# An encoder block on one core: seven products for more pieces of the third group, and adding transfers that read from memory

## The chip, the cores and the metric

The kernel runs on 1 core of one Trainium2 chip. The metric is the device time in microseconds of one execution; lower is better.

## The reference

One layer of a streaming encoder for 256 tokens with 2048 features, all in float32:

```python
x = x + 0.5 * swiglu(rms_norm(x, ffn1_norm), ffn1_w_up, ffn1_w_down)     # FFN1, d_ff = 5632
h = rms_norm(x, mix_norm); proj = h @ w_in                               # HGRN2 and RG-LRU branches
...
x = x + merged @ w_out
x = x + cross_attention(rms_norm(x, xattn_norm), rms_norm(mem, mem_norm), wq, wkv, wo)
x = x + 0.5 * swiglu(rms_norm(x, ffn2_norm), ffn2_w_up, ffn2_w_down)     # FFN2, d_ff = 5632
return rms_norm(x, final_norm)

def swiglu(h, w_up, w_down):
    gate, up = jnp.split(h @ w_up, 2, axis=-1)
    return (jax.nn.silu(gate) * up) @ w_down
```

The change touches the two FFNs and the start of the first.

## The kernel before

**Products in three matmuls.** TensorE multiplies in a float32 of reduced precision (fp32r). Each operand is split in two parts, h (the rounded value) and l (what rounding took off), and a product is h·h + l·h + h·l: three matmuls of 128x128 by 512 columns (`three`). A plain split of a 128x2048 piece of weights (1 MB, tile `raw`) is an ACT copy into `h` and a DVE subtraction into `l` (`split`).

**The FFN's tiles.** The 5632 hidden columns go in 11 groups of 512 (g = 0 to 10). The up weights of a group come in 8 pieces (p = 0 to 7), each with gate and up columns for two of x's 16 row blocks; x's matching operands are `pairs[p]`. A piece takes 8 products in the plain or the "mixed" form. The "fast" form is Strassen's scheme in Winograd's arrangement with 7 products; it needs sums and differences of x (made once, `sums`, on DVE and ACT) and of the weights: DVE makes `td` (three subtractions: 1024, 512 and 512 columns), then both `raw` (1536 columns) and `td` (twice 1024 columns) are split, into `h`, `l` and `th`, `tl`. Before the change groups 1 and 2 alternate mixed and fast; groups 3 to 10 go in the order p = 1, 3, 0, 4, 2, 6, 5, 7 with 0 and 6 mixed. After each group stand 2 or 4 "down" pieces, 24 matmuls each, which multiply hidden columns of earlier groups and add to the residual x.

**Adding transfers.** In groups 3 to 10 a mixed piece's split is kept off DVE (kind "added"): ACT writes -raw, rounded, into `l`, and a DMA from POOL's queue adds raw to it in SBUF, which leaves what rounding took off. `begin_added` does this one piece ahead, before the piece between; `prepare` later copies `raw` into `h`:

```python
sp.dma_start(raw, src)
act.activation(l, raw, ACT.Copy, scale=-1.0)
nc.gpsimd.dma_start(l, raw, accum_op=ALU.add)
```

**Order and buffers.** `weights` makes each piece ready two pieces before PE uses it. SP issues all loads in order. Each engine works through its instructions in the order that a scheduler fixes when the kernel is built, and an instruction that waits keeps all behind it on its engine. `raw`, `h` and `l` have three buffers each (a fast piece takes two of `h`), `td` and `tl` one; `slots` are 24 buffers of 128x1024 that hold x's operands, hidden operands and small things. The first 8 pieces have an order written out by hand (`tc.manual_schedule`); the lists `head` and `rest` put x's loads, x's sums and the residual's loads between the pieces.

**The start.** ACT's queue loads the gains (`vt`), PE runs 16 products of ones to be warm, ACT scales x by the gain into `xg`, and `split` makes x's operands from that.

Of the kernel before, what the change touches and what calls it, by code (L numbers as in the profile page):

```python
# [8 lines left out]
F32 = mybir.dt.float32  # L9
# [4 lines left out]
P = 128  # L14
T = 256
# [26 lines left out]
def ffn_order():  # L42

    out, down = [("plain", 0, p) for p in range(8)], [("down", 0, 1, c, 0) for c in range(4)]
    for g in range(1, NG):
        if g < 3:  # L50
            out += [(("mixed", "fast")[p % 2], g, p) for p in (0, 1, 2, 3, 5, 4, 7, 6)]
        else:
            out += [("mixed" if p in (0, 6) else "fast", g, p) for p in (1, 3, 0, 4, 2, 6, 5, 7)]
        if g > 2 and g % 2:
            down = [("down", g - 2, 2, c, b) for c in range(4) for b in (g - 2, g - 1)]
        n = 2 if g < 3 else 4
        out, down = out + down[:n], down[n:]
    return out + [("down", NG - 2, 2, c, b) for c in range(4) for b in (NG - 2, NG - 1)]
# [3 lines left out]
def block_kernel(ctx: ExitStack, tc: tile.TileContext, xT, xin, memT, vec, gfin, bgate, lruw, wu1, wd1, win, wv,  # L62
# [33 lines left out]

    vt = const.tile([P, NVEC], F32, name="vt")
    small_n = VEC["ident"][0]
    act.dma_start(vt[:, :small_n], vec[:, :small_n])

    def col(name, i=0, n=1):
        a = VEC[name][0] + i
        return vt[:, a:a + n]
# [1 line left out]
    ones = const.tile([P, P], F32, name="ones")  # L105
    dve.memset(ones, 1.0)
    warm = bank("warm")
    for _ in range(16):
        pe.matmul(warm[:, :P], ones, ones, start=True, stop=True)
    eps = const.tile([P, 1], F32, name="eps")  # L110
    act.activation(eps, ones[:, :1], ACT.Copy, scale=EPS)
# [6 lines left out]

    def split(h, l, raw):
        done["high"] = act.activation(h, raw, ACT.Copy).ins  # L120
        dve.tensor_tensor(out=l, in0=raw, in1=h.bitcast(F32), op=ALU.subtract)  # L121
# [64 lines left out]
    def begin_added(src):  # L186

        raw = rawp.tile([P, 2048], F32, name="raw", tag="raw")
        l = lp.tile([P, 2048], F32R, name="l", tag="l")
        sp.dma_start(raw, src)  # L190
        act.activation(l, raw, ACT.Copy, scale=-1.0)
        nc.gpsimd.dma_start(l, raw, accum_op=ALU.add)
        return raw, l

    def prepare(src, kind, cuts=1):
# [17 lines left out]
        dve.tensor_tensor(out=two[0], in0=raw[:, None, :512].broadcast_to([P, 2, 512]), in1=two[1], op=ALU.subtract)  # L213
        dve.tensor_tensor(out=td[:, 1024:1536], in0=raw[:, 1024:1536], in1=td[:, :512], op=ALU.subtract)
        dve.tensor_tensor(out=td[:, 1536:], in0=raw[:, 1536:], in1=td[:, 1024:1536], op=ALU.subtract)
        h, l = split_tiles()
        split(h[:, 512:], l[:, 512:], raw[:, 512:])
        th = hp.tile([P, 2048], F32R, name="h", tag="h")
# [184 lines left out]
    BOTH = [2, 4]  # L403
    xd = []

    def operand_pairs(src, gain, q, xg, out):

        for a in src:
            i = len(out)
            g = xg[:, i * 512:(i + 1) * 512]  # L410
            for z in range(2):
                act.activation(g[:, z * T:][:, :T], a[:, z * T:(z + 1) * T], ACT.Copy,
                               scale=col(gain, 4 * q + 2 * i + z))
            h, l = slot(F32R, "xh"), slot(F32R, "xl")
            split(h[:, :512], l[:, :512], g)
# [8 lines left out]
        def sums():  # L424
            s = slot(name="xs")
            for i, ((h, l), less) in enumerate(out):
                a = [xg[:, i * 512 + j * P:][:, :P] for j in range(4)]

                def made(h, l, n, at, terms):
                    o = [s[:, at + j * P:][:, :P] for j in range(n)]  # L430
                    for j, (x, y, op) in enumerate(terms(o)):
                        dve.tensor_tensor(out=o[j], in0=x, in1=y, op=op)
                    split(h, l, s[:, at:at + n * P])

                if less:
                    made(*less, 2, 0, lambda o: ((a[0], a[1], ALU.subtract), (a[2], a[3], ALU.subtract)))
                if i or 2 * q in BOTH:
                    if not i:
# [15 lines left out]
    def part(pair, i, n):  # L454
        return [v[:, i * n:(i + 1) * n] for v in pair]
# [9 lines left out]
    def ffn(name, pairs, sq, then, begin=(), sums=()):  # L465
# [38 lines left out]
        for at, e in enumerate(order):  # L504
# [3 lines left out]
            if kind != "down":  # L508
# [3 lines left out]
                for i, (a, b, n) in enumerate(PRODUCTS[kind]):  # L512
                    u = uses[g, n]
                    if u[0] == (p, i):
                        accs[n] = bank()
                    own, less = pairs[p]
                    products.append((accs[n], part(own, a, P) if a >= 0 else part(less, -1 - a, P), part(w[b // 4] if fast else w, b % 4, 512),
                                     u[0] == (p, i), u[-1] == (p, i)))
# [53 lines left out]
    def head_x(p):  # L572

        q = p // 2
        if p % 2 == 0:
            xq[q] = slot(name="xf"), slot(name="xg"), []
        src, xg, out = xq[q]
        a = p % 2 * 512
        sp.dma_start(src[:, a:a + 512], xT[:, p * 512:(p + 1) * 512])
        sums = operand_pairs([src[:, a:a + 512]], "ffn1_norm", q, xg, out)  # L580
        if p % 2:
            sums1.append(sums)
        pairs1.append(out[-1])
# [51 lines left out]
    def to_mix(c, t):  # L635
        sq2.add(c, [t])
        if t == 0:
            return
        if c == 0:
            with tc.issue_after(done["residual"]):  # L640
# [539 lines left out]
```

## Time and profile before

| what | value |
|---|---|
| median of 3 runs | 2455.2 us (2454.61 to 2457.94) |
| the profiled execution's own time | 2454.05 us |
| its span, first to last instruction | 2452.3 us |
| PE, DVE, ACT busy | 2436.5, 1887.3, 1402.5 us |
| granted TensorE clock | 0.999 |
| HBM read | 472.07 MB, 193 GB/s over the span |
| FFN1, middle, FFN2 | about 0 to 700, 700 to 1745, 1745 to 2452 us |

Profile rows give the line of the source (L449: line 449 of the kernel before), the engine, the operation, output and input tiles, a count, the busy time, the mean of one and then the idle time of the engine ahead of them with what ended it. In the FFN, L449 is h·h, L450 l·h (x's low part) and L452 h·l (the weights' low part). `l<-raw` on POOL's queue is the adding transfer. Ends of matmuls are modelled; a row of them shows their rate better than the length of one.

### The profile page before, as it was taken

The page shows a single profiled execution, that of the slowest core. Times are in us where ns is not written, and L with a number is a line of the kernel's source. Part 1 is how long each engine was busy: PE and PEld are TensorE (multiplying, and loading weights), DVE is VectorE, ACT ScalarE, POOL GpSimd, SP SyncE. Part 2 cuts the span into 40 slices and gives each one's busy share as a digit, 9 for nine tenths or more (in the row PEclk, how much of TensorE's full clock was granted, in tenths as well). Part 3 has the DMA queues.
Part 4 walks back from the last instruction along what each step waited for, and adds up shares of the span by engine and source line. Part 5 has one row for each costly group of instructions (what it writes and reads, how often), then busy time and mean ns, then how long its engine had stood idle before and what let it go on. Part 6 is the DMA issues. An engine that isn't in the chain of part 4 may idle for free.

```text
span 2452.3 us, 30292 instructions
## 1 busy us (share of the span) xinstructions
PE 2436.5 (99%) x12250; PEld 2032.2 (83%) x12250; DVE 1887.3 (77%) x2015; ACT 1402.5 (57%) x1399; POOL 28.1 (1%) x36
## 2 busy tenths in 40 slices
PE   9999999999999999999999999999999999999998
PEld 8787888888888888888888888888888788888887
DVE  7989999999865757577665676556689999999995
ACT  8566666666564454477434554555555666666664
POOL 0000000000000000000000000000000000000000
PEclk9999999999999999999999999999999999999999
DMA  7567777777655544546555555444555777777774
GB/s 288 196 219 228 239 232 234 238 238 239 229 187 189 174 173 179 177 168 230 189 189 178 210 197 189 172 172 155 189 189 185 230 240 238 240 240 234 233 237 153
DMA packets 75308, 509.69 MB, mean 208 GB/s; under 512 B 8352, under 2 KB 8608, under 8 KB 15264
## 3 DMA queue, kind: packets, MB, share of 16 engines
q1 hardware_dynamic: 69840, 473.06, 54.7%
q0 software_dynamic: 4608, 33.56, 6.6%
q8 instruction: 96, 1.57, 0.3%
q10 hardware_dynamic: 720, 1.13, 0.1%
q14 instruction: 44, 0.36, 0.0%
HBM read 472.07 MB, written 2.10 MB: 193 GB/s over the span
## 4 chain that ended last, share of the span: by engine, by line
PE 92%; DMA 3%; DVE 3%; issue 1%; ACT 1%; SPq 0%; ACTq 0%; POOLq 0%; DVEq 0%
PE acc L452 16%; PE acc L449 16%; PE acc L450 16%; PE acc L231 11%; PE acc L252 8%; PE acc L253 8%; PE acc L255 8%; PE acc L235 5%; DMA raw<-wu 2%; DVE l L121 1%; DMA l<-raw 1%; PE acc L488 1%; ACT h L120 1%; PE acc L389 1%; DVE tl L121 0%
## 5 line engine op out<-in xcount | busy, mean ns | idle before, releaser
L121 DVE TENSOR_TENSOR l<-raw,h 128x2048 fp32r<-128x2048 f32 (+2 forms) x420 | 873.9, 2084 | 327.0 <-ACT h L120 322.4
L120 ACT ACTIVATE h<-raw 128x2048 fp32r<-128x2048 f32 (+2 forms) x420 | 734.8, 1752 | 534.7 <-PE acc L253 205.3
L449 PE MATMUL acc<-h,xh 128*128 128x512 f32 x1280 | 500.3, 391 | 4.3 <-ACT h L120 4.2
L450 PE MATMUL acc<-h,xl 128*128 128x512 f32 x1280 | 497.7, 389 | 0.0
L120 ACT ACTIVATE h<-td 128x1024 fp32r<-128x1024 f32 x224 | 235.8, 1055 | 241.4 <-DVE td L213 98.8
L121 DVE TENSOR_TENSOR tl<-td,h 128x1024 fp32r<-128x1024 f32 x224 | 273.1, 1221 | 82.6 <-ACT h L120 51.4
L252 PE MATMUL acc<-h,ops 128*128 128x512 f32 x832 | 326.9, 393 | 0.0
L253 PE MATMUL acc<-h,ops 128*128 128x512 f32 x832 | 324.3, 390 | 0.0
L449 PEld LDWEIGHTS acc<-h,xh 128*128 128x128 f32 x1280 | 240.3, 188 | 59.0 <-ACT h L120 8.4
L450 PEld LDWEIGHTS acc<-h,xl 128*128 128x128 f32 x1280 | 240.4, 188 | 49.1
L231 PE MATMUL acc<-ops,h 128*128 128x512 f32 x1152 | 277.9, 393 | 0.3
L449 PE MATMUL acc<-h,hidop 128*128 128x512 f32 x704 | 275.9, 392 | 0.0
L450 PE MATMUL acc<-h,hidop 128*128 128x512 f32 x704 | 274.4, 390 | 0.0
L231 PEld LDWEIGHTS acc<-ops,h 128*128 128x128 f32 x1152 | 211.9, 188 | 42.8 <-DVE ops L292 0.9
L452 PE MATMUL acc<-l,xh 128*128 128x512 f32 x832 | 217.7, 389 | 0.0
L255 PE MATMUL acc<-l,ops 128*128 128x512 f32 x832 | 206.1, 390 | 0.0
L452 PE MATMUL acc<-l,hidop 128*128 128x512 f32 x704 | 188.4, 389 | 0.0
L255 PEld LDWEIGHTS acc<-l,ops 128*128 128x128 f32 x832 | 156.2, 188 | 32.4
L452 PEld LDWEIGHTS acc<-l,xh 128*128 128x128 f32 x832 | 156.0, 188 | 32.5 <-DVE l L121 0.2
L252 PEld LDWEIGHTS acc<-h,ops 128*128 128x128 f32 x832 | 156.3, 188 | 32.3
L253 PEld LDWEIGHTS acc<-h,ops 128*128 128x128 f32 x832 | 156.3, 188 | 31.6
L452 PEld LDWEIGHTS acc<-l,hidop 128*128 128x128 f32 x704 | 132.2, 188 | 27.7
(218 smaller groups left out, 2360.0 us busy)
## 6 DMA issues: line engine op xcount, KB each, us to landing
raw<-wu SPq DMA_DIRECT2D x172, 1024.0 KB, 5.3
raw<-wd SPq DMA_DIRECT2D x88, 1024.0 KB, 4.8
raw<-win SPq DMA_DIRECT2D x40, 1024.0 KB, 4.8
l<-raw POOLq DMA_DIRECT2D x32, 1024.0 KB, 11.0
raw<-wg SPq DMA_DIRECT2D x32, 1024.0 KB, 4.8
raw<-wab SPq DMA_DIRECT2D x16, 1024.0 KB, 4.8
raw<-wout SPq DMA_DIRECT2D x16, 1024.0 KB, 4.8
raw<-wq SPq DMA_DIRECT2D x16, 1024.0 KB, 4.8
```

Source lines behind the costliest of these rows:

```text
L120: done["high"] = act.activation(h, raw, ACT.Copy).ins
L121: dve.tensor_tensor(out=l, in0=raw, in1=h.bitcast(F32), op=ALU.subtract)
L231: pe.matmul(acc, h[:, k * P:(k + 1) * P], xs[k], start=k == 0, stop=False)
L235: done["product"] = pe.matmul(acc[:, :T], l[:, k * P:(k + 1) * P], xs[k][:, :T], start=False, stop=k == KT - 1).ins
L252: pe.matmul(accs[t], x[:, t * P:][:, :P], h[j], start=first and j == 0, stop=False)
L253: pe.matmul(accs[t], x[:, T + t * P:][:, :P], h[j], start=False, stop=False)
L255: done["product"] = pe.matmul(accs[t], x[:, t * P:][:, :P], l[j], start=False, stop=last and j == 3).ins
L389: pe.transpose(accs[m // 2][:, m % 2 * T + t * P:][:, :P], tile[:, t * 512 + m * P:][:, :P], ident)
L449: pe.matmul(acc, ah, bh, start=start, stop=False)
L450: pe.matmul(acc, al, bh, start=False, stop=False)
L452: pe.matmul(acc, ah, bl, start=False, stop=stop)
L488: pe.transpose(acc[:, z * T + t * P:][:, :P], hid[t][:, (2 * y + z) * P:][:, :P], ident)
```

## The change

- Group 2 takes the order and forms of groups 3 to 10: two mixed pieces and six fast ones.
- An adding transfer reads the weights from HBM and no longer from `raw`. It is begun by the preparation of the piece two ahead of it, after that piece's first splits, and its `h` is made there too, as two tiles of 1024 columns in `slots`. All mixed pieces are done so but (1,0), (1,6) and (2,0), so two of group 1 and one of group 2 are new: 38 adding transfers where 32 were.
- The gains' load is cut in two (16 columns first), 13 warm products stand where 16 did, x's first operand is made directly from x and the gain, and the second half of each of x's scalings goes to DVE in the first FFN. x's sums for pairs 2 and 4 are made at pieces 16 and 17 (the two downs after group 1). `parameters` is held back behind the latest weight copy.

```diff
-        if g < 3:
+        if g < 2:
             out += [(("mixed", "fast")[p % 2], g, p) for p in (0, 1, 2, 3, 5, 4, 7, 6)]
...
-    act.dma_start(vt[:, :small_n], vec[:, :small_n])
+    first_n = VEC["mix_norm"][0]
+    for a, b in ((0, first_n), (first_n, small_n)):
+        act.dma_start(vt[:, a:b], vec[:, a:b])
...
-    for _ in range(16):
+    for _ in range(13):
...
-            kind = "fast" if e[0] == "fast" else "added" if e[0] == "mixed" and e[1] > 2 else "plain"
+            kind = "fast" if e[0] == "fast" else "plain"
+            if e[0] == "mixed" and e[1:] not in ((1, 0), (1, 6), (2, 0)):
+                kind = "added"
...
-            if plan and plan[0][2] == "added":
-                begun.append(begin_added(plan[0][1]))
-            ahead.append((k, prepare(src, kind, 4 if i < 4 else 1)))
+            begin = [p[1] for p in plan[1:2] if p[2] == "added"]
+            ahead.append((k, prepare(src, kind, 4 if i < 4 else 1, begin)))
...
         act.activation(l, raw, ACT.Copy, scale=-1.0)
-        nc.gpsimd.dma_start(l, raw, accum_op=ALU.add)
-        return raw, l
+        nc.gpsimd.dma_start(l, src, accum_op=ALU.add)
+        h = [slot(F32R, "wh") for _ in range(2)]
+        for i in range(2):
+            done["high"] = act.activation(h[i], raw[:, i * 1024:(i + 1) * 1024], ACT.Copy).ins
+        return h, [l[:, :1024], l[:, 1024:]]
...
         if kind == "added":
-            raw, l = begun.pop(0)
-            h = hp.tile([P, 2048], F32R, name="h", tag="h")
-            done["high"] = act.activation(h, raw, ACT.Copy).ins
-            return h, l
+            return begun.pop(0)
...
         split(h[:, 512:], l[:, 512:], raw[:, 512:])
+        begun.extend(begin_added(b) for b in begin)
         th = hp.tile([P, 2048], F32R, name="h", tag="h")
...
+                act.activation(h[:, :T], a[:, :T], ACT.Copy, scale=by[0])
+                dve.tensor_scalar(out=h[:, T:512], in0=a[:, T:], scalar1=by[1], scalar2=None, op0=ALU.mult)
+                for z in range(2):
+                    dve.scalar_tensor_tensor(out=l[:, z * T:(z + 1) * T], in0=a[:, z * T:(z + 1) * T], scalar=by[z],
+                                             in1=h[:, z * T:(z + 1) * T].bitcast(F32), op0=ALU.mult, op1=ALU.subtract)
+                later.append(scaled)
...
-        rest[i] = lambda q=q: sums1[q]()
+        rest[i] = lambda q=q: sums1[q](((0, "less"), (1, "sums")))
+    def late_sums(q):
+        with tc.issue_after(done["low"]):
+            sums1[q](((0, "sums"),))
+
+    for q, i in ((1, 16), (2, 17)):
+        rest[i] = lambda q=q: late_sums(q)
```

More of the change, by code (lines that the diff above doesn't have):

```diff
@@ L120, in split @@
         done["high"] = act.activation(h, raw, ACT.Copy).ins
-        dve.tensor_tensor(out=l, in0=raw, in1=h.bitcast(F32), op=ALU.subtract)
+        done["low"] = dve.tensor_tensor(out=l, in0=raw, in1=h.bitcast(F32), op=ALU.subtract).ins
     def split_tiles():
@@ L191, in begin_added, with prepare @@
         act.activation(l, raw, ACT.Copy, scale=-1.0)
[L192 to L195 removed]
+        nc.gpsimd.dma_start(l, src, accum_op=ALU.add)
[3 more added lines that the diff above has]
+        return h, [l[:, :1024], l[:, 1024:]]
+    def prepare(src, kind, cuts=1, begin=()):
         if kind == "added":
[L198 to L201 removed]
+            return begun.pop(0)
         raw = rawp.tile([P, 2048], F32, name="raw", tag="raw")
@@ L217, in prepare @@
         split(h[:, 512:], l[:, 512:], raw[:, 512:])
+        begun.extend(begin_added(b) for b in begin)
         th = hp.tile([P, 2048], F32R, name="h", tag="h")
@@ L404, in block_kernel, with operand_pairs @@
     xd = []
-    def operand_pairs(src, gain, q, xg, out):
+    def operand_pairs(src, gain, q, xg, out, later=None):
         for a in src:
@@ L410, in operand_pairs, with scaled @@
             g = xg[:, i * 512:(i + 1) * 512]
-            for z in range(2):
-                act.activation(g[:, z * T:][:, :T], a[:, z * T:(z + 1) * T], ACT.Copy,
-                               scale=col(gain, 4 * q + 2 * i + z))
             h, l = slot(F32R, "xh"), slot(F32R, "xl")
-            split(h[:, :512], l[:, :512], g)
+            def scaled(g=g, a=a, i=i):
+                by = [col(gain, 4 * q + 2 * i + z) for z in range(2)]
+                act.activation(g[:, :T], a[:, :T], ACT.Copy, scale=by[0])
+                if later is None:
+                    act.activation(g[:, T:], a[:, T:], ACT.Copy, scale=by[1])
+                else:
+                    dve.tensor_scalar(out=g[:, T:], in0=a[:, T:], scalar1=by[1], scalar2=None, op0=ALU.mult)
+            if later is None or 2 * q + i:
+                scaled()
+                split(h[:, :512], l[:, :512], g)
+            else:
+                by = [col(gain, 4 * q + 2 * i + z) for z in range(2)]
+                act.activation(h[:, :T], a[:, :T], ACT.Copy, scale=by[0])
[4 more added lines that the diff above has]
+                later.append(scaled)
             less = None if i else (h[:, 512:768], l[:, 512:768])
@@ L422, in operand_pairs, with sums @@
             out.append(((h, l), less))
-        def sums():
+        def sums(which=((0, "less"), (0, "sums"), (1, "less"), (1, "sums"))):
             s = slot(name="xs")
@@ L433, in made @@
                     split(h, l, s[:, at:at + n * P])
-                if less:
+                if less and (i, "less") in which:
                     made(*less, 2, 0, lambda o: ((a[0], a[1], ALU.subtract), (a[2], a[3], ALU.subtract)))
-                if i or 2 * q in BOTH:
-                    if not i:
+                if (i or 2 * q in BOTH) and (i, "sums") in which:
+                    if not i and len(which) > 1:
                         s = slot(name="xs")
@@ L516, in ffn @@
                     own, less = pairs[p]
-                    products.append((accs[n], part(own, a, P) if a >= 0 else part(less, -1 - a, P), part(w[b // 4] if fast else w, b % 4, 512),
-                                     u[0] == (p, i), u[-1] == (p, i)))
+                    x = part(own, a, P) if a >= 0 else part(less, -1 - a, P)
+                    if fast:
+                        y = part(w[b // 4], b % 4, 512)
+                    elif isinstance(w[0], list):
+                        y = part([v[b // 2] for v in w], b % 2, 512)
+                    else:
+                        y = part(w, b, 512)
+                    products.append((accs[n], x, y, u[0] == (p, i), u[-1] == (p, i)))
                 three(products)
@@ L579, in head_x @@
         sp.dma_start(src[:, a:a + 512], xT[:, p * 512:(p + 1) * 512])
-        sums = operand_pairs([src[:, a:a + 512]], "ffn1_norm", q, xg, out)
+        later = []
+        sums = operand_pairs([src[:, a:a + 512]], "ffn1_norm", q, xg, out, later)
+        if later:
+            rest[1] = later[0]
         if p % 2:
@@ L639, in to_mix @@
         if c == 0:
-            with tc.issue_after(done["residual"]):
+            with tc.issue_after(done["residual"]), tc.issue_after(done["high"]):
                 parameters()
```

## The prediction

> **What bounds the kernel now.** I read the page's busy shares, then the table of PE's waits, then the stages, then the chain and the DMA answers.
>
> ```profile
> PE 2436.5 (99%) x12250; PEld 2032.2 (83%) x12250; DVE 1887.3 (77%) x2015; ACT 1402.5 (57%) x1399; POOL 28.1 (1%) x36
> PE acc L449 <- ACT h L120: 4.2, 5, 1.7
> PE acc L452 <- DVE tl L121: 1.2, 2, 1.0
> PE warm L109 <- DVE ones L106: 1.1, 1, 1.1
> PE acc L488 <- DVE ev L481: 0.2, 1, 0.2
> 50.00:100.00 50.00, 46.95 (x207) 37.16 (x206) 48.93 (x62) 32.42 (x32) 0.00 (x0) 1.00 0.53 190
> 100.00:150.00 50.00, 50.00 (x223) 40.57 (x222) 46.15 (x43) 26.31 (x22) 0.00 (x0) 1.00 0.56 195
> 150.00:200.00 50.00, 48.16 (x215) 39.02 (x214) 44.70 (x49) 30.35 (x27) 1.86 (x2) 1.00 0.70 217
> 300.00:350.00 50.00, 50.00 (x225) 41.18 (x224) 45.66 (x45) 31.12 (x25) 1.72 (x2) 1.00 0.68 228
> ```
>
> In the stage rows the columns after the length are PE, PEld, DVE and ACT busy. PE is the bound: its four kinds of wait sum to 6.7 us of 2452.3, the granted clock stays at 1.00, and at 300 to 350 PE has no gap at all. But it is a balanced bound: in the FFN's stages DVE is busy 44.7 to 48.9 of every 50 us. So there are two ways to gain (fewer matmuls, or the 5.6 us of waits behind the start) and much to lose, since any new wait of PE adds to the end in full.
>
> **The matmuls.** The rate comes from the chain's rows of a row of eight:
>
> ```profile
> 111.67 1.82 PE acc L452 x8
> 113.48 0.87 PE acc L488 x8
> 157.20 1.91 ACT l L191
> 159.43 11.66 DMA l<-raw
> 171.15 4.72 DMA raw<-wu
> 2.12 5.15 DMA raw<-wu
> ```
>
> One 512-column matmul takes 1.82/8 = 0.227 us. A fast piece (7 products of 3) is 21 of them, 4.8 us; a mixed, plain or down piece 24, 5.4 us. The third group (g=2) goes from 4 mixed and 4 fast to 2 and 6, from 60 products to 58: 2 x 3 = 6 matmuls less in each FFN, 12 in all, **-2.7 us**, straight on PE.
>
> **The start.** Columns: start, length.
>
> ```profile
> 1.05 6.44 PE L109 MATMUL warm<-ones 128*128 128x128 f32 x32 [1.05 <-DVE ones L106]
> 4.26 0.21 ACT L616 ACTIVATE par<-vt 128x8 f32<-128x8 f32 x1 [1.59 <-DMA vt<-vec]
> 4.61 0.89 ACT L412 ACTIVATE xg<-xf,vt 128x256 f32<-128x256 f32 x2
> 5.53 0.63 ACT L120 ACTIVATE xh<-xg 128x512 fp32r<-128x512 f32 x1
> 6.07 2.50 ACT L120 ACTIVATE h<-raw 128x512 fp32r<-128x512 f32 x4
> 7.25 0.48 PE L449 MATMUL acc<-h,xh 128*128 128x512 f32 x1
> ```
>
> PE runs its 16 warm products without a gap until 7.25, and x and the first weights are made by 6.7. With 13, the warm ones end 3 x 6.2/16 = 1.2 us earlier, near 6.1. On ACT the two parameter rows, one scaling and the extra copy fall out ahead of the first weight quarter (0.35 + 0.45 + 0.5, about 1.3 us), so the data are there by about 5.5: the warm products still end last. The third quarter lands at 2.12 + 5.15 = 7.3, and PE wants it 8 matmuls after 6.1, at 7.9, one 0.6 us copy later: just in time. **-1.1 us**. That x's pairs are scaled half on DVE, and the first scaled tile made later, is work moved under an engine that waits for loads there: nothing. The parameters move to the end of the FFN under PE's work: nothing.
>
> **DVE and ACT work.** Rows from 130 to 700 us (busy, mean ns, then the idle before):
>
> ```profile
> L120 ACT ACTIVATE h<-td 128x1024 fp32r<-128x1024 f32 x99 | 104.4, 1055 | 102.4 <-PE acc L450 41.3 <-DVE td L213 36.8 <-DVE td L215 24.2
> L120 ACT ACTIVATE h<-raw 128x1536 fp32r<-128x1536 f32 x49 | 72.9, 1487 | 31.4 <-PE acc L450 18.6 <-issue 10.9 <-DMA raw<-wu 1.1
> L191 ACT ACTIVATE l<-raw 128x2048 fp32r<-128x2048 f32 x16 | 30.6, 1910 | 14.1 <-DMA raw<-wu 14.0
> L121 DVE TENSOR_TENSOR tl<-td,h 128x1024 fp32r<-128x1024 f32 x100 | 122.1, 1222 | 37.1 <-ACT h L120 24.6 <-PE acc L452 11.3
> L121 DVE TENSOR_TENSOR l<-raw,h 128x2048 fp32r<-128x2048 f32 x45 | 102.8, 2284 | 7.6 <-ACT h L120 7.6
> L121 DVE TENSOR_TENSOR l<-raw,h 128x1536 fp32r<-128x1536 f32 x49 | 85.8, 1750 | 0.7 <-ACT h L120 0.7
> L213 DVE TENSOR_TENSOR td<-raw 128x1024 f32<-128x1024 f32 x49 | 59.9, 1222 | 1.3
> L215 DVE TENSOR_TENSOR td<-raw,td 128x512 f32<-128x512 f32 x50 | 34.3, 687 | 0.7
> ```
>
> A fast piece costs DVE 1.22 + 2 x 0.69 + 1.75 + 2 x 1.22 = 6.8 us against PE's 4.8; a plain one 2.3; an adding one none. The second group (g=1) changes two plain pieces into adding ones, DVE -4.6. The third has two fast pieces more and three plain splits less: 13.6 - 6.9 = +6.7, while PE gets 1.4 shorter. Also the sums of x's pairs 2 and 4 come from the head (where DVE had 48.93 of 50) into the two down pieces between these groups. So the first waits (1.0 on tl, 1.7 on h) lose their reason, and the third group, 46.15 + 6.7 = 52.9 in 50 us, gets a new one: about +3 per FFN.
>
> **The adding transfer, where the sum is decided.** Before, POOL adds raw from SBUF, so raw stays taken until the transfer lands: the chain has it, 159.43 + 11.66 and then the load at 171.15, and 1.84 us of PE are lost in that stage. Now it reads the weights from HBM; two ACT passes into slots free raw at once. But the begin is no earlier for the tile that gates it: l still has three buffers and its order of allocation is the same, so ACT's negation still stands behind PE's end of the piece that had the buffer. What is earlier is the *load of the next adding piece*, and it now meets the transfer.
>
> ```profile
> l<-raw POOLq DMA_DIRECT2D x32, 1024.0 KB, 11.0
> raw<-wu SPq DMA_DIRECT2D x172, 1024.0 KB, 5.3
> q0 software_dynamic: 75, 0.61, 98.7%
> q1 hardware_dynamic: 16, 0.07, 6.3%
> raw<-wu SPq DMA_DIRECT2D x1, 1024.0 KB, 6.6
> raw<-wu SPq DMA_DIRECT2D x1, 1024.0 KB, 8.5
> ```
>
> The last four: the queues' shares and SP's only load of 245 to 248 us, where a transfer begun at 240.6 is under way, and SP's load begun 0.45 us behind a transfer at 1895.6. In the first window the added data hold all 16 engines for 98.7%, and the load issued then waits until they are done: it lands 6.6 us after issue, some 2 us behind the transfer. The Trainium skill, "DMA: Bandwidth & Descriptors", section "Queues, rings and completion order", has each engine drain a whole packet from one queue before it turns to the next; the two shares agree.
>
> Now ACT's built order in the changed kernel. In about every other group from the fourth on it is: first half of the second fast piece's th (h<-td), h of the next fast piece, *first wh of the second adding piece*, then the second half of that th. The wh waits for its load, and everything behind it waits too. Count from T, the issue of the first adding transfer. PE: T is 1.9 + 0.1 us after PE leaves the third down piece; the fourth down takes 5.4, eight transposes 0.9, the first fast piece 4.8, and 10 matmuls (2.3) of the second are possible without the second half: T + 11.4. ACT: the load, issued near T + 3 (a th pass, two hidop and two wh passes free its buffer), lands 2.1 behind the transfer's 11.0: T + 13.1; wh 1.06 and h 1.06 make T + 15.2. **PE waits 3.8 us.** In the other groups the order puts h of the seventh piece ahead of the fifth's second th half; its load is issued 0.9 behind the second transfer and lands with it at about T' + 10.5; h 1.49 and h 1.06 make T' + 13.0, and PE is there at T' + 11.3 (rest of a fast piece 0.6, mixed 5.4, fast 4.8, less 1.8 for the two passes that lie ahead of T', plus 2.3): 1.7 us. Eight groups of each kind in the two FFNs: 30 + 14 = **+44**.
>
> The bounds: if the load lands 6.6 after its issue, at T + 9.6, the half is there at T + 11.7 and only 0.3 is left; if it lands with nothing shared it costs 0. If two loads slip ahead of the transfer, as at 159.65 where one did and it took 11.7, it lands 2.5 later and the long wait is 6. I take 3.8, nearest to the 98.7% window.
>
> The second group has adding transfers for the first time, with no downs between them: for p=4 it is begun when PE has some 10 us to go to its l; 11.0, or 13.5 behind two loads, is 1 to 4 us late: +3, and +1 for the other FFN.
>
> **The sum**, against the profiled execution's own 2454.05 (span 2452.3; the median is 2455.2): -2.7 - 1.1 - 4.5 (old waits: 1.0 + 1.7 + 1.8) + 44 + 4 + 2 x 3 = +46, so **2500**.
>
> **Rivals.**
> *Shared engines*: the load lands 8.5 after issue (the last row), T + 11.5, long wait 2.2, short 0.5: 8 x 2.7 = 22, and 8 for the early groups: 2454 - 8.3 + 30 = 2476. For it: that row. Against: the 98.7%.
> *All hidden, faster*: the load lands before T + 9.3, so that ACT never keeps PE; DVE catches up in the third group out of the 4 to 5 us of spare on both sides: 2454 - 8.3 = 2446. It decides at T + 9.3. For it: PE has no wait in 300 to 350 now. The Trainium skill's fit for such a transfer (same page, section "Anatomy of one DMA — SWDGE (gpsimd) path", 2.0 us and the bytes at 436 GB/s) would make it some 4.4 us as an estimate, which would give this case; the row says 11.0, so it isn't followed.
> *DVE alone*: the transfers are hidden, but the third group's DVE work is not: 2446 + 2 x 6 = 2458.
>
> **Numbers.** Forecast 0.62 (2480 to 2524, the top from the long wait of 6), shared 0.20 (2462 to 2480), DVE alone 0.08, all hidden 0.08, above 0.02. The range of 2462 to 2524 holds 0.82. Same is within 0.2% (4.9 us), about what can be told from no change: half of DVE alone and some, 0.05; faster 0.08; slower 0.87.
>
> **What would show it.** Right: PE's waits for ACT h grow from 4.2 to 40 or more, 2 to 5 us at one place in nearly every group from the fourth on; ACT's idle time ahead of wh, by the load, is large; the chain holds DMA raw<-wu and l<-wu through both FFNs; matmuls of L449's line fall by 4. Wrong: landings of l<-wu near 5, or PE without gaps in the middle of an FFN.

## The result and the profile after

| | median | range | runs |
|---|---|---|---|
| before | 2454.9 us | 2454.46 to 2457.94 | 4 |
| after | 2549.4 us | 2546.55 to 2551.56 | 4 |

The ratio is 1.0381, 95% interval 1.0363 to 1.0399: slower, as forecast, but by 94 us and not by 46, and above the range of 2462 to 2524. The profiled execution has a span of 2547.7 us (2452.3 before) at a mean granted clock of 0.985 (0.999 before). One run of the fifth experiment below took 3478.9 us at a granted clock of 0.654; its ratio leaves that run out, its median does not (2470.2 us without it).

The page of the changed kernel: busy time, the chain by engine, and the DMA rows (KB each, median us from issue to landing).

```profile
PE 2469.2 (97%) x12232; PEld 2046.6 (80%) x12232; DVE 1902.3 (75%) x2039; ACT 1406.5 (55%) x1443; POOL 33.4 (1%) x42
PE 79%; DMA 9%; DVE 6%; ACT 4%; issue 1%; SPq 0%; ACTq 0%; DVEq 0%
...
l<-wu POOLq DMA_DIRECT2D x38, 1024.0 KB, 12.0
```

PE has 18 records fewer (12 matmuls of the FFNs, 3 warm products of two records each) and yet 32.7 us more busy time. DMA holds 9% of the chain (3% before). PE's waits (us in total, times, longest) and four stages (length, PE, PEld, DVE, ACT, POOL busy, clock, DMA share, GB/s):

```profile
PE acc L472 <- ACT h L122: 57.5, 20, 4.9
PE acc L475 <- DMA l<-wu: 6.5, 2, 5.1
...
50.00:100.00 50.00, 42.86 (x173) 33.53 (x172) 39.17 (x54) 32.71 (x34) 1.88 (x2) 0.90 0.69 217
...
150.00:200.00 50.00, 48.33 (x212) 38.17 (x211) 49.18 (x52) 32.13 (x29) 1.76 (x2) 1.00 0.69 205
300.00:350.00 50.00, 45.91 (x195) 37.29 (x194) 39.76 (x40) 26.25 (x24) 1.76 (x2) 0.93 0.67 210
```

L472, L473 and L475 are the old L449, L450 and L452. Waits for ACT's h went from 4.2 to 57.5 us. In the stage at 300 to 350, PE lost 4.09 us to idleness, but it did 195 matmuls where 225 were done before: 30 fewer are 6.8 us of work at 0.227. The other 2.7 us are in the clock column, 0.93 where 1.00 stood. That column, which is 0.90 at 50 to 100, is what the forecast had no term for. At 150 to 200 DVE is busy 49.18 of 50, and PE still loses less there than at 300 to 350.

One of the long waits. First ACT's timeline (start, length, line, operation, then the idle time ahead of it and what ended it), then the issues of the two transfers and PE's row, then two stretches of time around it.

```profile
586.50 1.06 ACT L198 ACTIVATE wh<-raw 128x1024 fp32r<-128x1024 f32 x1 [4.84 <-DMA raw<-wu]
587.47 1.04 ACT L122 ACTIVATE h<-td 128x1024 fp32r<-128x1024 f32 x1
```

```profile
572.72 0.87 POOL L195 DMA_DIRECT2D l<-wu  x1 [48.25 <-DVE td L219]
575.19 0.33 SPq L193 DMA_DIRECT2D raw<-wu  x1
...
588.56 0.80 PE L472 MATMUL acc<-h,xh 128*128 128x512 f32 x1 [4.94 <-ACT h L122]
```

```profile
586.20:593.00 6.80, 4.44 (x11) 3.52 (x12) 3.84 (x4) 4.00 (x4) 0.00 (x0) 0.50 0.15 64
593.00:596.40 3.40, 3.40 (x16) 2.84 (x15) 1.23 (x1) 3.40 (x4) 0.86 (x1) 0.99 0.46 113
```

With T = 572.72, the issue of the adding transfer, the forecast's times are met almost to the letter. The next adding piece's load is issued at T + 2.5 (forecast T + 3). It lands by 586.50, T + 13.8 (forecast 13.1). The half of th that PE needs ends at 588.51, T + 15.8 (forecast 15.2), and PE ran out near 583.6, T + 10.9 (forecast 11.4): 4.94 us of waiting. In all of the changed kernel ACT is idle for 43.7 us ahead of `wh` copies, in 13 places, until their load lands. But the clock falls to half while PE waits, and PE's next 4.44 us of work take that long only because of it: 11 matmuls, and in the 3.40 us behind them 16.

### The profile page after: what moved, and what is told of

It reads as the page before. It is cut to its first block, busy times and chain, and to the rows that moved or that the text cites. A ratio compares the mean times of both kernels' runs of the same rounds, so it can differ in the third digit from the quotient of the medians.

```text
span 2547.7 us, 30239 instructions
## 1 busy us (share of the span) xinstructions
PE 2469.2 (97%) x12232; PEld 2046.6 (80%) x12232; DVE 1902.3 (75%) x2039; ACT 1406.5 (55%) x1443; POOL 33.4 (1%) x42
## 3 DMA queue, kind: packets, MB, share of 16 engines
q1 hardware_dynamic: 69840, 473.06, 51.2%
## 4 chain that ended last, share of the span: by engine, by line
PE 79%; DMA 9%; DVE 6%; ACT 4%; issue 1%; SPq 0%; ACTq 0%; DVEq 0%
PE acc L475 13%; PE acc L472 12%; PE acc L473 12%; PE acc L236 10%; DMA raw<-wu 8%; PE acc L257 7%; PE acc L258 7%; PE acc L260 7%; PE acc L240 5%; ACT h L122 2%; DVE l L123 2%; ACT wh L198 1%; DVE tl L123 1%; DVE td L217 1%; PE acc L511 1%
## 5 line engine op out<-in xcount | busy, mean ns | idle before, releaser
L123 DVE TENSOR_TENSOR l<-raw,h 128x2048 fp32r<-128x2048 f32 (+2 forms) x414 | 857.9, 2077 | 370.4 <-ACT h L122 348.3
L122 ACT ACTIVATE h<-raw 128x2048 fp32r<-128x2048 f32 (+2 forms) x414 | 719.7, 1742 | 496.5 <-PE acc L258 206.2
L472 PE MATMUL acc<-h,xh 128*128 128x512 f32 x988 | 394.4, 400 | 57.8 <-ACT h L122 57.5
L122 ACT ACTIVATE h<-td 128x1024 fp32r<-128x1024 f32 x232 | 244.1, 1053 | 320.4 <-DVE td L217 236.7
L473 PE MATMUL acc<-h,xl 128*128 128x512 f32 x988 | 389.2, 395 | 0.0
L123 DVE TENSOR_TENSOR tl<-td,h 128x1024 fp32r<-128x1024 f32 x232 | 282.2, 1221 | 112.7 <-ACT h L122 76.4
L472 PEld LDWEIGHTS acc<-h,xh 128*128 128x128 f32 x988 | 188.0, 190 | 110.2 <-ACT h L122 72.3
L472 PE MATMUL acc<-h,hidop 128*128 128x512 f32 x704 | 276.1, 392 | 0.0
L473 PE MATMUL acc<-h,hidop 128*128 128x512 f32 x704 | 274.5, 390 | 0.0
L475 PE MATMUL acc<-l,xh 128*128 128x512 f32 x820 | 222.6, 397 | 8.0 <-DMA l<-wu 6.5
L473 PEld LDWEIGHTS acc<-h,xl 128*128 128x128 f32 x988 | 188.5, 191 | 37.4
L475 PEld LDWEIGHTS acc<-l,xh 128*128 128x128 f32 x820 | 156.3, 191 | 43.5 <-DMA l<-wu 7.4
L475 PE MATMUL acc<-l,hidop 128*128 128x512 f32 x704 | 188.5, 389 | 0.0
L475 PEld LDWEIGHTS acc<-l,hidop 128*128 128x128 f32 x704 | 132.2, 188 | 27.6
```

The source lines that it names most:

```text
L123: done["low"] = dve.tensor_tensor(out=l, in0=raw, in1=h.bitcast(F32), op=ALU.subtract).ins
L472: pe.matmul(acc, ah, bh, start=start, stop=False)
L473: pe.matmul(acc, al, bh, start=False, stop=False)
L475: pe.matmul(acc, ah, bl, start=False, stop=stop)
```

## The experiments

Each experiment was run beside the kernel before on one chip. The chips of the batches differ; the kernel before had medians of 2454.5 to 2455.7 us on them. The first four add or undo one thing in the changed kernel, the next four do one part alone in the kernel before, and the last four follow from them. The theory: a copy into `wh` that waits for a late load stands in ACT's queue ahead of a split that PE needs, and most of these waits are paid twice, once as waiting and once as half clock.

**1. Fill the wait with work (the clock's part).** At four places of each FFN, 15 matmuls by a tile of zeros go ahead of the sixth product of the second fast piece, on operands that are there. They add nothing to the result.

```diff
+            if i == 5:
+                for _ in range(fill):
+                    pe.matmul(products[0][0], zeros, products[0][2][0], start=False, stop=False)
...
-                three(products)
+                three(products, 15 if kind == "fast" and g in (5, 7, 9, 10) and p == 3 else 0)
```

> The changed kernel, with 15 matmuls against a tile of zeros (they add nothing to a sum that is open anyway) put ahead of the sixth product of the second fast piece in groups 5, 7, 9 and 10 of both FFNs, where PE waits 4.0 to 5.1 us for ACT's copy: 8 places, 3.4 us of PE work each, inside the wait. Clock theory: the waits end when they did, but PE is no longer idle for over 3 us at these places, so most of the low-clock stretches that follow them (3.4 or 6.8 us each at half clock, 44 us in all in the changed kernel's records) are gone: 2549 - 20, about 2527 to 2532, with PE's waits for ACT down by some 27 us. Rival, that PE's extra busy time has another cause (contention on SBUF, say): the matmuls fit into the wait and nothing changes, 2549, or they come on top, up to 2549 + 27.

Measured 2530.1 us, ratio 1.0305 (1.0290 to 1.0321). The waits table, and the stretch of the wait above:

```profile
PE acc L478 <- ACT h L122: 27.1, 18, 3.2
...
586.00:593.00 7.00, 7.00 (x32) 5.78 (x32) 4.20 (x5) 5.32 (x5) 0.53 (x1) 1.00 0.39 131
```

120 useless matmuls made the kernel 19 us faster. They fill time in which PE had nothing to do, so without the clock they could gain nothing; with PE kept running the clock stays at 1.00 there. PE's waits for h fell by 30.4 us, and the useless matmuls took 120 x 0.227 = 27.2 of that, so less waiting gave some 3 us. The rest is the clock: without the useless matmuls PE's busy time fell by 18.9 us (2469.2 to 2477.5 less 27.2), while between the start and the tail the time at half clock fell by 47.8, from 71.7 to 23.9. That the clock is a large separate part of the loss is shown.

**2. One piece ahead again.** The early copy into `wh` stays.

```diff
-            begin = [p[1] for p in plan[1:2] if p[2] == "added"]
-            ahead.append((k, prepare(src, kind, 4 if i < 4 else 1, begin)))
+            if plan and plan[0][2] == "added":
+                begun.append(begin_added(plan[0][1]))
+            ahead.append((k, prepare(src, kind, 4 if i < 4 else 1)))
```

> The changed kernel with one thing undone: the adding transfer and its wh copies are begun one piece ahead, in front of that piece's preparation, as in the kernel before; the source stays HBM, the copies stay early, the seven products and the start stay. Queue theory (a wh copy that waits for a load held behind a transfer stands on ACT in front of a th half that PE needs): the order on ACT changes, the long waits of groups 5, 7, 9 and 10 go, and with them the clock's part: 2460 to 2480. Source theory (the transfer from HBM takes 12.0 where 11.0 were, and loads suffer): nothing changes, about 2549. Seven-products theory: 2540 or more.

**3. The copy made late again.** The begin stays two pieces ahead.

```diff
-        h = [slot(F32R, "wh") for _ in range(2)]
-        for i in range(2):
-            done["high"] = act.activation(h[i], raw[:, i * 1024:(i + 1) * 1024], ACT.Copy).ins
-        return h, [l[:, :1024], l[:, 1024:]]
+        return raw, l
...
-            return begun.pop(0)
+            raw, l = begun.pop(0)
+            h = hp.tile([P, 2048], F32R, name="h", tag="h")
+            done["high"] = act.activation(h, raw, ACT.Copy).ins
+            return h, l
```

> The changed kernel, but the high part of an adding piece is made when the piece itself is prepared, by one ACT copy into a buffer of h, as before; transfer still two pieces ahead and from HBM. Queue theory: ACT's early waits for the load are left to the negation alone, so the long waits go: 2455 to 2470, still above 2455 for the third group's DVE work (1 to 3 us at two places of each FFN) less the 12 matmuls. Source theory: about 2549. If it is the place of the beginning alone: about 2549 too.

Measured 2483.0 us, ratio 1.0114 (1.0099 to 1.0129), for the second and 2465.8 us, ratio 1.0044 (1.0029 to 1.0059), for the third. The waits of the one, then of the other:

```profile
PE acc L473 <- ACT h L122: 20.8, 13, 4.7
```

```profile
PE acc L472 <- ACT h L122: 7.9, 6, 3.9
```

Each alone gives most of the loss back (66 and 84 of 94 us), so the loss needs both. The early begin by itself is harmless: with it in place and the early copies gone the waits for h are 7.9 us. This points at the copy and not at the transfer, but doesn't part them cleanly: without the early copies `raw` is held longer, loads come at other times, and the adding transfer's median falls from 12.0 to 10.6 us. The ninth experiment parts them. One piece ahead came out 3 us above its range: 13 waits remain there, and four stretches at half clock.

**4. The source back in SBUF.**

```diff
-        nc.gpsimd.dma_start(l, src, accum_op=ALU.add)
+        nc.gpsimd.dma_start(l, raw, accum_op=ALU.add)
```

> The changed kernel with the adding transfer reading raw in SBUF again. raw then stays taken until the transfer lands, so the second adding piece's load starts later but meets no transfer. Queue theory: one long wait per odd group becomes several short ones of about 1.4 us; the waits in all stay near 60 us, but each is too short for the clock to fall: 2500 to 2525. Source theory: the waits fall to what they were before, about 2455.

Measured 2543.8 us, ratio 1.0352 (1.0334 to 1.0369): 19 us above the expected range. The source makes little difference. The waits, two of PE's rows, and the stretch right behind them:

```profile
PE acc L472 <- ACT h L122: 60.2, 47, 3.6
...
599.48 0.50 PE L472 MATMUL acc<-h,xh 128*128 128x512 f32 x1 [1.06 <-ACT h L122]
...
601.80 0.58 PE L472 MATMUL acc<-h,xh 128*128 128x512 f32 x1 [1.12 <-ACT h L122]
...
602.10:605.50 3.40, 3.40 (x9) 2.65 (x8) 3.33 (x4) 0.42 (x1) 0.00 (x0) 0.50 0.94 311
```

The 20 waits became 47 shorter ones, many of about 1.1 us. I had expected those to leave the clock alone. But the trace has 12 stretches at half clock, 51.2 us together. Most stand behind single waits of 1.8 to 3.6 us that are still there; a few, like the one shown, stand behind two shorter waits close together.

**5. The third group alone.** The kernel before with group 2 in the other groups' order, and nothing else.

```diff
-        if g < 3:
+        if g < 2:
```

> The kernel before with one edit: the third group takes the order of the later ones, with six fast pieces and two plain ones; nothing else. Matmul theory: 12 matmuls of 0.227 us less, 2452. DVE theory: DVE gets 6.7 us more work in a stage where it was busy 46 of 50 us (and here two mixed pieces stay plain splits), so PE waits at two or three places of 1 to 3 us in and behind this group in each FFN: +12 - 2.7, about 2460 to 2468.

Measured 2470.8 us, ratio 1.0061 (1.0048 to 1.0074): 2 to 3 us above the range.

```profile
PE acc L449 <- ACT h L120: 10.4, 10, 2.8
PE acc L452 <- DVE tl L121: 2.6, 7, 1.0
PE acc L452 <- DVE l L121: 2.3, 2, 1.2
PE acc L488 <- DVE hidop L493: 1.5, 2, 0.8
...
182.60 9.48 DMA raw<-wu
...
194.66 0.51 PE acc L449
```

The last two are rows of the chain: the longest wait, 2.82 us before 194.66, is a load of 9.48 us that a fast piece waits for. The waits for DVE in these rows are 6.4 us where 1.4 were before, those for ACT's h 10.4 where 4.2 were. Twelve matmuls less (2.7 us) don't pay for that. In the changed kernel one of the two mixed pieces of this group is an adding piece; here both are plain.

**6. The start alone.** The split load of the gains, 13 warm products, x's first operand made directly, the second halves of x's scalings on DVE, the parameters later. x's sums stay where they were, so the later sums of pairs 2 and 4 were not run by themselves. (Two of the edits:)

```diff
-    for _ in range(16):
+    for _ in range(13):
...
+    first_n = VEC["mix_norm"][0]
+    for a, b in ((0, first_n), (first_n, small_n)):
+        act.dma_start(vt[:, a:b], vec[:, a:b])
```

> The kernel before with the start's edits alone: gains in two loads, 13 warm products, x's first operand made directly, second halves of x's scalings on DVE, the parameters held back; x's sums where they were, groups and transfers as before. If the lead of 1.1 us survives: 2454. If the waits at the second group (1.0 for tl, 1.7 for h), which end by DVE's work and not by the start, take it back, and DVE has eight scalings more: 2455 to 2458.

Measured 2458.6 us, ratio 1.0013 (1.0005 to 1.0022), just above what was expected. The first product comes earlier, as forecast (6.30 in the changed kernel, 7.25 before), and a wait of 1.9 us at 59 takes it back, with the clock. Which of the start's edits makes that wait was not tested.

```profile
PE acc L471 <- ACT h L122: 7.1, 6, 1.9
...
58.00:62.20 4.20, 1.71 (x7) 0.84 (x7) 4.00 (x6) 4.17 (x6) 0.00 (x0) 1.00 0.00 0
62.20:65.60 3.40, 3.40 (x13) 2.92 (x12) 3.02 (x5) 3.35 (x5) 0.00 (x0) 0.50 0.94 308
```

**7 and 8. More adding pieces alone, the source alone.** The kernel before with the five mixed pieces of groups 1 and 2 other than (1,0), (1,6) and (2,0) made as adding pieces, and the kernel before with only the transfer's source changed.

```diff
-            kind = "fast" if e[0] == "fast" else "added" if e[0] == "mixed" and e[1] > 2 else "plain"
+            kind = "fast" if e[0] == "fast" else "plain"
+            if e[0] == "mixed" and e[1:] not in ((1, 0), (1, 6), (2, 0)):
+                kind = "added"
```

```diff
-        nc.gpsimd.dma_start(l, raw, accum_op=ALU.add)
+        nc.gpsimd.dma_start(l, src, accum_op=ALU.add)
```

> The kernel before with one edit: the mixed pieces 2 and 4 of group 1 and 2, 4 and 6 of group 2 become adding ones, begun one piece ahead and from SBUF as before. Queue theory: the transfer itself does no harm where its copies stand behind the work that PE needs; DVE is rid of 5 splits of 2.3 us per FFN in the stage where it was fullest, so the waits of 1.7 and 1.8 us go: 2450 to 2452, faster than both kernels. If an adding transfer costs as such (engines held for 5 us each): 2456 or more.

> The kernel before with the adding transfer's source changed from raw in SBUF to the weights in HBM, nothing else: 32 MB more of HBM reads, and raw free once ACT has copied it. Queue theory: no harm, the one wait of 1.8 us behind the first transfer of FFN1 may go: 2452 to 2456. Source theory: the transfers take longer and PE waits for them: above 2460.

Measured 2453.0 us, ratio 0.9991 (0.9982 to 0.9999), and 2451.8 us, ratio 0.9986 (0.9978 to 0.9995): two small gains, near what was expected (the first 1 us less than forecast).

**9. The begin moved behind the splits.** The direct test of the queue: copies, transfer and two pieces ahead all stay, and only the place in the queues changes, for the negation and the transfer's issue as for the copies.

```diff
         split(h[:, 512:], l[:, 512:], raw[:, 512:])
-        begun.extend(begin_added(b) for b in begin)
         th = hp.tile([P, 2048], F32R, name="h", tag="h")
         tl = scoped["tl"].tile([P, 2048], F32R, name="tl", tag="tl")
         for a in (0, 1024):
             split(th[:, a:a + 1024], tl[:, a:a + 1024], td[:, a:a + 1024])
+        begun.extend(begin_added(b) for b in begin)
```

> The changed kernel with one thing moved: the adding piece that is begun two pieces ahead is begun behind the fast piece's own splits in the program, not between its load and its splits. Its plain load, its two copies on ACT and its adding transfer stay, and stay two pieces ahead; only their place in ACT's and POOL's queues changes. Queue theory (a copy that waits for a held load stands ahead of the split that PE needs): PE's waits for ACT's h, 57.5 us in 20 waits in the changed kernel, fall under 20 us, no more than four stretches at half clock are left, and the time is 2465 to 2485. Rival (the transfer begun two pieces ahead is itself too much beside the other loads, wherever the copies stand): the waits stay above 45 us and the time above 2530.

Measured 2486.8 us, ratio 1.0129 (1.0115 to 1.0143); 62 us come back. The waits, and ACT's timeline ahead of the longest of those that stay:

```profile
PE acc L472 <- ACT h L122: 18.9, 9, 4.4
...
1892.09 1.48 ACT L122 ACTIVATE h<-raw 128x1536 fp32r<-128x1536 f32 x1 [4.73 <-DMA raw<-wu]
```

The queue theory holds for two thirds of the loss: 57.5 us of waits become 18.9, though the adding transfers are no faster (a median of 12.1 us where 12.0 were). The time is 2 us above its range, and five stretches at half clock stay where at most four were expected. What stays is a late load: here ACT waits 4.73 us for a fast piece's own load. This part is not one of place on ACT, and what makes that load late was not tested.

**10. Both undone.** Edits 2 and 3 together.

> The changed kernel with both parts of the early begin undone: one piece ahead, and the copy made in one when the piece is prepared. What stays of the change: the third group's seven products for six pairs, its other order of kinds with more adding pieces, the adding transfer reading from HBM, and the start. The parts run alone against the kernel before gave +16.1 (third group with its two groups' kinds), +3.3 (start), -2.3 (more adding pieces) and -3.2 (source); if they add up, the time is 2455.7 + 16.1 + 3.3 - 3.2 = 2472 or, since late_copy alone gave 2465.8, 2463 to 2473. If begin_one_ahead and late_copy took away separate waits, it is below 2460.

Measured 2466.7 us, ratio 1.0045 (1.0031 to 1.0059), the same as the third. By their ratios the four parts done alone gave +15.0 + 3.2 - 2.2 - 3.4 = +12.6 us, a little other than the figures in the expectation; this is +11.0, within the intervals. (The later sums of x's pairs 2 and 4 are in this kernel and in none of the four.) So the early begin and the early copy together cost 2549.4 - 2466.7 = 83 us, and all the rest of the change 11 to 12. The largest wait left is again behind a late load of a fast piece: at 1932.56 ACT has waited 4.39 us for it.

**11 and 12. What gained, together.** Edits 7 and 8 in the kernel before; and the same with two of the start's edits, the gains' load in two and 14 warm products. x's first operand, scalings and sums and the parameters are there as in the kernel before, so the twelfth kernel does not have "the start of the changed kernel", as the second expectation says.

```diff
+    first_n = VEC["mix_norm"][0]
+    for a, b in ((0, first_n), (first_n, small_n)):
+        act.dma_start(vt[:, a:b], vec[:, a:b])
...
-    for _ in range(16):
+    for _ in range(14):
```

> The kernel before with two things that each gained a little alone: adding pieces in place of plain ones in the second group too (-2.3 us alone) and the adding transfer reading from HBM (-3.2 us alone). If the two gains are of separate waits they add up: 2449 to 2451 beside 2455. If both take away the same waits: 2452 to 2453.

> The same with the start of the changed kernel, and beside it the gains' load in two, so that the first pair's gain lands ahead of the rest, and 14 warming products in place of 16. The changed start alone was 3.3 us slower than before because of a wait near 59 us that dropped the clock; if that wait came of the old kinds there, this is 2447 to 2450; if it comes of the start, 2452 to 2455.

Measured 2452.9 us, ratio 0.9993 (0.9984 to 1.0002), and 2450.9 us, ratio 0.9984 (0.9975 to 0.9993). The two gains don't add up: together they can't be told from no change. With these two edits of the start 3.6 us are gained on the kernel before, the best of all versions, and the interval excludes 1. The time lies between the two readings and decides neither, since most of the start isn't in it. PE's largest waits in it:

```profile
PE acc L512 <- DVE hidop L517: 1.3, 2, 0.7
...
PE acc L476 <- DVE tl L123: 1.0, 1, 1.0
...
```

No wait for ACT's h is left, and the largest that there is takes 1.3 us in two places. No stretch at half clock is left between the start and the tail.

## Why the prediction was right about the sign and wrong about the size

**The step that failed: "the granted clock stays at 1.00".** The forecast read this from the kernel before, whose waits are 1.8 us at most, and priced each new wait at its own length; the sum has no term for a slower clock behind the waits. The profile's clock record has 14 stretches at half clock between the start and the tail of the changed kernel, 71.7 us together, all of 3.4 or 6.8 us and each at one of PE's new waits. (The first and one of the last; the columns are those of the stages.)

```profile
64.00:67.40 3.40, 3.33 (x12) 2.93 (x13) 3.26 (x8) 2.07 (x4) 0.00 (x0) 0.50 0.51 217
...
2316.80:2320.20 3.40, 3.40 (x8) 2.75 (x9) 3.33 (x4) 0.13 (x1) 0.00 (x0) 0.50 0.41 166
```

Where all of a stretch is PE's work, half of it is lost. The account of the span: it grew by 95.4. PE's idle time, span less busy, went from 15.8 to 78.5, +62.7. PE's busy time went up by 32.7, and since 12 matmuls (2.7 us) and three warm products (1.2) fell away, the same matmuls took 36.6 more. In the 14 stretches PE was busy for 58.3 us, and half of that, 29 us, is the clock. The other 7 are not put down to a cause; the third experiment's trace has some 6 us of such an excess in all, with one stretch of 3.4 us at half clock. So of the 49 us by which the forecast fell short some 29 are the clock, some 7 are open, and some 13 are waits that were sized too small. The clock's part may be less: among the four runs of the changed kernel the granted clock goes from 0.984 to 0.988, some 20 us of half clock, and the time from 2551.6 to 2546.6, so there, as an estimate, 1 us at half clock cost a quarter of a us and not a half. Later waits may take some of it up; no run shows that.

The Trainium skill, "TensorE: Matmul & The Clock Gate", section "Part 1: The HAM clock gate (the "warmup" mystery)", says that the array falls to half rate after an idle window of about 3.4 us, and that it takes a busy window of about 3.4 us to come back, in windows that run freely. The lengths and the factor of two agree with the rows above. The length of the gap doesn't: 2.41 us before 2316.79 were enough, and so were two waits of 1.1 in the fourth experiment.

The traces say more. In each of the five that have several such stretches, all of them begin on one grid of 3.413 us: from 64.00 to 2316.80 above it is 660 steps. Five more traces have one stretch, and the grid can be laid through it. Cut into these steps, the ten traces have 46 falls from full to half clock. At full clock every step in which PE was idle for 1.94 us or more (33 of them) was followed by half clock, no step with less than 1.4 us idle was, and between the two it went either way. So what counts is how much of one step PE is idle, in one wait or in several. Three steps of the changed kernel, then two of the fourth experiment (the first two numbers are the step's length and PE's busy time):

```profile
2313.37:2316.78 3.41, 1.01 (x5) 0.51 (x3) 1.10 (x2) 2.43 (x2) 0.00 (x0) 1.00 1.01 428
1978.86:1982.27 3.41, 2.22 (x10) 1.50 (x8) 1.03 (x1) 0.98 (x1) 0.00 (x0) 1.00 0.99 375
1982.27:1985.68 3.41, 1.91 (x8) 1.61 (x9) 2.88 (x2) 1.45 (x2) 0.00 (x0) 1.00 0.85 353
```

```profile
2042.50:2045.91 3.41, 1.70 (x8) 1.08 (x6) 0.83 (x1) 1.12 (x1) 0.00 (x0) 1.00 0.95 356
2045.92:2049.33 3.41, 2.06 (x9) 1.69 (x10) 2.99 (x3) 1.30 (x2) 0.00 (x0) 1.00 0.68 286
```

The wait of 2.41 us lies in one step, and half clock follows. The wait of 2.69 us before 1983.77 falls on two steps, 1.19 and 1.50, and nothing follows; neither does it behind a wait of 3.08 us in the fourth experiment, which falls on two steps as 1.7 and 1.4.

**The waits: places right, lengths a little short.** PE's rows with a wait for h from the fourth group of the first FFN to its end (the last bracket is the wait), and some of the second:

```profile
204.47 0.50 PE L472 MATMUL acc<-h,xh 128*128 128x512 f32 x1 [2.47 <-ACT h L122]
253.98 0.50 PE L472 MATMUL acc<-h,xh 128*128 128x512 f32 x1 [2.76 <-ACT h L122]
321.41 0.80 PE L472 MATMUL acc<-h,xh 128*128 128x512 f32 x1 [4.09 <-ACT h L122]
404.17 0.51 PE L472 MATMUL acc<-h,xh 128*128 128x512 f32 x1 [1.74 <-ACT h L122]
455.26 0.50 PE L472 MATMUL acc<-h,xh 128*128 128x512 f32 x1 [4.00 <-ACT h L122]
536.59 0.50 PE L472 MATMUL acc<-h,xh 128*128 128x512 f32 x1 [1.24 <-ACT h L122]
657.77 0.71 PE L472 MATMUL acc<-h,xh 128*128 128x512 f32 x1 [4.57 <-ACT h L122]
...
1925.27 0.79 PE L472 MATMUL acc<-h,xh 128*128 128x512 f32 x1 [3.83 <-ACT h L122]
1983.77 0.50 PE L472 MATMUL acc<-h,xh 128*128 128x512 f32 x1 [2.69 <-ACT h L122]
...
2316.79 0.80 PE L472 MATMUL acc<-h,xh 128*128 128x512 f32 x1 [2.41 <-ACT h L122]
```

With the 4.94 us shown above, four are long and four short, and the second FFN has as many from 1983.77 on: eight of each, as forecast. By place they are ten and six: in the fifth group (g = 4) the wait stands at the second fast piece, where the long ones are, but is short (2.76 and 1.93 us). The long ones are 3.8 to 4.9 us, 33.9 in all, where eight of 3.8 were put down; the short ones are 1.2 to 2.8 us, 16.6 in all, where eight of 1.7 were. The term of 44 was 50.5.

**The early groups, forecast at +4 and +6.** An adding transfer of the second group is late at the place that was forecast, by 5.1 us where 1 to 4 were put down, and only in the first FFN. The third group's DVE term was too small: alone, and with one plain split more, the group costs 15 us with its share of clock, not the 3.3 that 6 less 2.7 makes. It is not DVE alone either: more than half of its new waits are for ACT's h, the longest behind a late load. And the wait of 3.83 us at 1925.27, in the second FFN's early groups, wasn't on the list.

**The start.** -1.1 was forecast and 0.95 seen at the first product. That these agree is in part luck: the profile's clock record begins at full clock at 6.55 us in the kernel before, at 5.95 in the changed one and at 4.16 in the start alone, and there the first product came at 5.44. What "nothing" missed is a wait near 59 us, 1.9 us with half clock behind it, and some shorter ones: PE's waits grow from 6.7 to 10.3 us, and the gain is a loss of 3 us when the start is alone.

**The rivals.** All hidden (2446), DVE alone (2458) and shared engines (2476) are out for the change as a whole: the waits stand where the forecast put them and are no shorter. But the reason that was given for the late load, that the adding data hold all engines until they are done, is wrong. In the kernel before, the load behind the 98.7% was issued at 246.77, and its queue moved nothing from 246.2 to 248.9 (the first two rows): it had not begun yet, and the 6.3% were the end of an earlier load, so those two shares say nothing of how queues take turns. In the changed kernel the load of 575.19 and the adding transfer shared the engines from 578.5 to 583.5, nearly packet for packet, 75 to 89 (the last three rows):

```profile
246.77 0.33 SPq L210 DMA_DIRECT2D raw<-wu  x1
...
q0 software_dynamic: 67, 0.55, 98.2%
...
q0 software_dynamic: 89, 0.73, 69.9%
q1 hardware_dynamic: 75, 0.61, 30.4%
...
raw<-wu SPq DMA_DIRECT2D x1, 1024.0 KB, 11.3
```

The load had less than a third of the engines' time there, took 11.3 us and landed 0.6 us behind the transfer (572.72 + 13.2). Where the forecast had it land 2.1 us behind a transfer of 11.0, the transfer took 13.2; that the two come out within 0.7 us of each other is in part luck. The rival of shared engines had the better mechanism, but put the landing at 8.5 us after issue. The Trainium skill's fit ("DMA: Bandwidth & Descriptors", section "Anatomy of one DMA — SWDGE (gpsimd) path"), which as an estimate gave 4.4 us for the adding transfer, stays contradicted: its rows have 12.0 here and 11.0 before.

**The range.** Its top was put down to long waits of 6 us. By the forecast's own sum that makes 2500 + 8 x 2.2 = 2518, not 2524; the result lies above both.

## What to carry to other kernels

Moving work earlier is free only if nothing in its engine's queue stands behind it: an instruction that waits for a late load holds everything after it, so a copy that isn't needed yet belongs behind the splits that are. Price a new wait of PE of 2 us or more at its length and up to half of the stretch at half clock that can follow, here 1.7 or 3.4 us more, and read the clock column of every stage, not the mean. Where PE must wait anyway, useless matmuls on operands that are there can be cheaper than silence.

## What the runs showed of the hardware that was not expected

- Half clock came in stretches of 3.4 and 6.8 us, after single waits of 1.9 us (at 64), 2.41 (at 2316.8) and 2.76 (at 254), and not after others of 2.47 (at 204.5), 2.69 (at 1983.8) and 3.08 (at 2047.3 in the fourth experiment). The length alone didn't decide; PE's idle time within one step of a fixed grid of 3.413 us did, from 1.94 us on.
- Two waits of about 1.1 us in one step had the same effect as one of 2 us.
- An adding transfer of 1 MB took a median of 11.0 us from SBUF in the kernel before and 10.9 from HBM where only the source was changed (the eighth experiment, the first row): the source by itself makes no difference. In the changed kernel it took 12.0 from HBM and 8.9 from SBUF (the fourth experiment, the second row), where `raw` is held longer and the loads come at other times. That the traffic beside it sets the time fits this, but was not tested by itself.

```profile
l<-wu POOLq DMA_DIRECT2D x32, 1024.0 KB, 10.9
...
l<-raw POOLq DMA_DIRECT2D x38, 1024.0 KB, 8.9
```
